# Feed-forward up projection as seven products of quadrants, with the down projection as a stage of its own

## The chip, the cores and the metric

The kernel runs on one core of a Trainium2 chip. The metric is the time of one execution on the device in microseconds (us). Three executions of the kernel before took 2954.87, 2956.52 and 2956.6 us (median 2956.52). All data are fp32. Each large matrix product is computed on TensorE from operands that are split into a high and a low part in the fp32r format: `a = ah + al`, `b = bh + bl`, and `ah*bh + ah*bl + al*bh` is summed in PSUM. One product of two tiles is therefore three matmuls.

## The reference

One layer of a transformer over 1024 tokens and 1024 channels: an input norm, a modulation, nine projections, a retention branch, a differential attention branch, their merge, and a feed-forward part. The change concerns the last part alone. Cut to that:

```python
def conv_ffn(h, w_up, conv_w, conv_b, w_down):
    u, gate = jnp.split(h @ w_up, 2, axis=-1)          # h 1024x1024, w_up 1024x5632
    u = dwconv_centred(u, conv_w, conv_b)              # 3 taps along the tokens
    return (jax.nn.gelu(u, approximate=False) * gate) @ w_down   # 2816x1024

x = layer_norm(alpha * x + g1 * y_mix, ln1_g, ln1_b)
y_ff = conv_ffn(x * (1 + sc2) + sh2, w_up, conv_w, conv_b, w_down)
x = layer_norm(alpha * x + g2 * y_ff, ln2_g, ln2_b)
```

## The kernel before

The kernel is a row of stages p0 to p6, each with pools of its own. A scheduler that works from a timeline of its own sets the order of the instructions on each engine; a semaphore wait stands wherever an instruction needs another engine's result. Engines are in order: an instruction that waits holds back what is queued behind it.

**Stage p5** (output projection, first norm). Tokens are taken in two halves `i` of 512 (four blocks of 128, `bb`) and channels in two halves `ch`. For each block, 24 matmuls `pxo` (8 channel tiles by 3) give 512 output channels. VectorE adds them to the residual (`r`, then `x0`). Once both channel halves of a block are there, `norm1` takes mean and variance on VectorE, a square root on ScalarE and a few one-column operations on VectorE; ScalarE normalises the 128x1024 block, TensorE transposes it in eight pieces (`pth`), and ScalarE copies them to `h32[i]`, the transposed input of the feed-forward part (channel tile `k` in 0 to 7, 512 tokens). When a half is complete, `hT[i][k]`, the split pair of `h32*scale + shift`, is made.

**Stage p6** (feed-forward). The 2816 inner channels are 22 tiles `f` of 128.

- `up(c0)` loads a 1024x128 block of `w_up` (`load_split`: a DMA into `wraw`, a ScalarE cast to `wh`, a VectorE subtraction to `wl`) and multiplies it with both token halves: 8 tiles by 3 by 2 halves = 48 matmuls of 512 columns into a PSUM tile of 1024 columns. `ff_tile(f)` calls it for the `u` block and for the gate block (96 matmuls), convolves and applies Gelu (two passes on ScalarE, two on VectorE, which read PSUM), multiplies with the gate, and splits the result into `fh`, `fl`.
- `down(fs)` loads the rows of `w_down` for two tiles (GpSimd multiplies them by the gate `g2`, the row `mrow`), and for eight token blocks and two column halves sums 12 matmuls `pyd` in one of two PSUM banks ("small"); VectorE adds the bank to the accumulator `acc[b]`, kept in SBUF. The last `down` takes four tiles at once, and `finish(b)` does the second norm and the store after each block.
- `down` of a pair of tiles runs between the `ff_tile` calls of the next pair, so the two projections are interleaved on TensorE.
- `init_acc` loads the normed input from DRAM (`d_x1`) into `acc` and has GpSimd multiply by `alpha*ln1_g` and add `ln1_b`: 16 operations of 128x1024. It is issued after the first `ff_tile`, and the up projection of the first tiles runs meanwhile.
- For the first two tiles `up` is called with `apart`: the first token half's matmuls stand ahead of the second half's, so that they can run before the second half is normed.

The weights go through a ring of 3 `wraw` and 4 pairs `wh`, `wl`. On the profile's page L256 is the matmul of `mm3`, L1230 that of `up` with `apart` off, L71 every `tensor_tensor`, L85 every cast, L81 every activation, L77 every `scalar_tensor_tensor`.

Of the kernel before, what the change touches and what calls it, by code (L numbers as in the profile page):

```python
# [8 lines left out]
F32 = mybir.dt.float32  # L9
# [55 lines left out]
def build(nc, tc, A, out, upto=99, dbg=None):  # L65
    top = ExitStack()
    V, S, G, PE, SP = nc.vector, nc.scalar, nc.gpsimd, nc.tensor, nc.sync
# [39 lines left out]
    d_oT = dram("d_oT", [HD, P, T])  # L107
    d_x1 = dram("d_x1", [T, D])
    d_tab = dram("d_tab", [HR, P, 896])

# [136 lines left out]

    def mm3(ps, lhs, rhs, n, start, stop, step=512):

        (wh, wl), (mh, ml) = lhs, rhs  # L250
        cuts = list(range(0, n, step))
        seq = [(wh, mh), (wh, ml), (wl, mh)]
        for i, (w, m) in enumerate(seq):
            for c in cuts:
                e = min(c + step, n)
                PE.matmul(ps[:, c:e], w, m[:, c:e], start=start and i == 0, stop=stop and i == 2)  # L256

# [560 lines left out]
    with ExitStack() as ph:  # L818
# [145 lines left out]
        for h in range(HR):  # L964
            nxt = prepare(h + 1) if h + 1 < HR else iter(())
            for c in range(NC):
# [14 lines left out]
                if h == HR - 1 and c == 2:  # L981
                    early.close()
                    open_ring("wring2", 3, 4, top, "right")
                    ws0 = w_cols(A["w_diff_out"][0], 0, 256)
# [5 lines left out]

    halves = top.enter_context(tc.tile_pool(name="halves", bufs=1))
    mrow = halves.tile([P, 2 * D], F32, name="mrow")
# [4 lines left out]
    ops = top.enter_context(tc.tile_pool(name="ops", bufs=1))  # L999
    open_big(top)  # L1000
# [109 lines left out]
    hs = misc.tile([P, 2, KT], F32, name="hs")  # L1110
    hT = []
    with ExitStack() as ph:
# [49 lines left out]
        for i in range(2):  # L1162
            for ch in range(2):
# [30 lines left out]
    with ExitStack() as ph:  # L1194
        wp = ph.enter_context(tc.tile_pool(name="p6", bufs=1))
        acc = half_pair("acc")
        acc = [acc[b // 4].rearrange("p k t -> p (k t)")[:, (b % 4) * D:(b % 4 + 1) * D] for b in range(8)]
        w_up = A["w_up"][0].rearrange("(k p) n -> p k n", p=P)
        w_dn = A["w_down"][0]

        def rows2(names):
            r = []
            for n in names:
                r.append(misc_tile("rows", 2 + len(r)))
                SP.dma_start(out=r[-1], in_=A[n].broadcast_to([P, D]))
            return r
# [10 lines left out]

        def up(c0, apart):

            h, l = load_split(w_up[:, :, c0:c0 + P])  # L1220
            pu = big_ps("pu")
            for i in range(2) if apart else (None,):
                for k in range(KT):
                    w = h[:, k * P:(k + 1) * P], l[:, k * P:(k + 1) * P]
                    if apart:
                        mm3(pu[:, i * 512:i * 512 + 512], w, hT[i][k], 512, k == 0, k == KT - 1)
                        continue
                    for at, (a, b) in enumerate(((0, 0), (0, 1), (1, 0))):
                        for j in range(2):
                            PE.matmul(pu[:, j * 512:j * 512 + 512], w[a], hT[j][k][b],  # L1230
                                      start=k == 0 and at == 0, stop=k == KT - 1 and at == 2)
            return pu

        def ff_tile(f):
            pu = up(f * P, f < 2)
            pg = up(FF + f * P, f < 2)
            cw = [pcol2[:, j * NF + f:j * NF + f + 1] for j in range(3)]
            u = misc_tile("u", f % 2)
            act(u, pu, AF.Identity, bias=pcol[:, V_CB + f:V_CB + f + 1], scale=cw[1])
            stt(u[:, 1:], pu[:, :T - 1], cw[0], u[:, 1:], ALU.mult, ALU.add)  # L1240
            stt(u[:, :T - 1], pu[:, 1:], cw[2], u[:, :T - 1], ALU.mult, ALU.add)
            act(u, u, AF.Gelu)
            tt(u, u, pg, ALU.mult)
            ah = wp.tile([P, T], F32R, name="fh", tag="fh", bufs=4)
            al = wp.tile([P, T], F32R, name="fl", tag="fl", bufs=4)
            split(ah, al, u)
            return ah, al

        def down(fs, acts, last):
            ws = [load_split(w_dn[f * P:(f + 1) * P, :], mul=mrow[:, D:]) for f in fs]  # L1250
            for b in range(8):
                cut = slice(b * P, b * P + P)
                for hf in range(2):
                    py = small_ps("pyd")
                    c = slice(hf * 512, hf * 512 + 512)
                    for i, (w, a) in enumerate(zip(ws, acts)):
                        mm3(py, (a[0][:, cut], a[1][:, cut]), (w[0][:, c], w[1][:, c]), 512, i == 0, i == len(fs) - 1)
                    tt(acc[b][:, c], py, acc[b][:, c], ALU.add)
                if last:
                    finish(b)  # L1260

        def finish(b):

            halves_of = [(slice(c, c + 512), acc[b][:, c:c + 512]) for c in (0, 512)]
            mv = wp.tile([P, 2], F32, name="mv2", tag="mv2", bufs=3)
            ln_mean_var(wp, [x for _, x in halves_of], mv, "ln2")
            if b < 7:
                rstd_shift(wp, mv[:, 0:1], mv[:, 1:2], 1, "ln2", 3)
            else:
                for c, x in halves_of:  # L1270
                    stt(x, x, mv[:, 0:1], l2[0][:, c], ALU.subtract, ALU.mult)
                rs = ln_rstd_root(wp, mv[:, 1:2], 1, "ln2s")
            for c, x in halves_of:
                if b < 7:
# [6 lines left out]

        pend = None
        for g in range(0, NF - 4, 2):
            a0 = ff_tile(g)
            if pend:
                down(*pend, False)
            else:
                with tc.issue_after(last):
                    init_acc()
            a1 = ff_tile(g + 1)  # L1290
            pend = ([g, g + 1], [a0, a1])
        g = NF - 4
        acts = [ff_tile(g)]
        down(*pend, False)
        l2 = rows2(("ln2_g", "ln2_b"))
        acts += [ff_tile(g + i) for i in range(1, 4)]
        down([g + i for i in range(4)], acts, True)
    return top

# [24 lines left out]
```

## Time and profile before

| | |
|---|---|
| median of three runs | 2956.52 us |
| the profiled execution's own time | 2954.79 us |
| its span, first to last instruction | 2953.0 us |
| TensorE busy | 2848.6 us, 96% of the span |
| VectorE, ScalarE, GpSimd busy | 1651.5, 968.3, 582.6 us |
| mean granted TensorE clock | 0.989 of full speed |
| first matmul of the up projection | 2194.16 us into the span |
| last matmul of the kernel | 2939.82 us |

The page counts a matmul from its issue to its end; matmuls are pipelined, so the distance between two starts is what one costs in a row. An idle time is put down to what ended it. "Chain" is the sequence of work that ended last, followed back from the end.

### The profile page before, as it was taken

To read this page: it belongs to the slowest core of one execution; us is meant where nothing else is said; L and a number is where in the kernel's file an instruction comes from. 1 tells how busy PE (TensorE), PEld (TensorE's weight loads), DVE (VectorE), ACT (ScalarE), POOL (GpSimd) and SP (SyncE) were. 2 spreads that over 40 slices of the span, in tenths; PEclk is the share of its full clock that TensorE was granted. 3 is DMA by queue.
4 is the path that set the end of the run, shared out by engine and by line. 5 is a ranking of instruction groups with operands and counts; after the bars stand their busy time and mean duration, and the time that the engine had idled before them with its cause. 6 is when DMAs were issued, how large, how long until landed. Compare 5 with 4: busy or idle time off the path is not lost.

```text
span 2953.0 us, 34822 instructions
## 1 busy us (share of the span) xinstructions
PE 2848.6 (96%) x13874; PEld 2378.6 (81%) x13874; DVE 1651.5 (56%) x2441; ACT 968.3 (33%) x1314; POOL 582.6 (20%) x407
## 2 busy tenths in 40 slices
PE   7999999999999999999988998999799999999998
PEld 5788888888888888888866777887677888888886
DVE  4853133200367767666689996476865444444446
ACT  4321100111354455544455544322344121112112
POOL 3321022100000000000055543233607000000014
PEclk9999999999999999999999999999999999999999
DMA  8554322422233323322143426657344111111111
GB/s 245 170 155 136 107 86 94 149 79 71 84 93 106 107 84 109 99 94 90 50 137 125 134 75 201 226 186 239 104 142 127 52 44 50 43 50 51 57 43 57
DMA packets 259170, 321.29 MB, mean 109 GB/s; under 512 B 14983, under 2 KB 192576, under 8 KB 259008
## 3 DMA queue, kind: packets, MB, share of 16 engines
q1 hardware_dynamic: 220704, 239.62, 26.3%
q10 hardware_dynamic: 38304, 79.45, 7.6%
q8 instruction: 109, 1.79, 0.3%
q14 instruction: 53, 0.43, 0.1%
HBM read 235.38 MB, written 83.62 MB: 108 GB/s over the span
## 4 chain that ended last, share of the span: by engine, by line
PE 83%; DVE 8%; DMA 4%; issue 2%; POOL 2%; ACT 1%; SPq 0%; DVEq 0%; POOLq 0%; ACTq 0%
PE pu L1230 15%; PE pg L256 12%; PE px L256 11%; PE pxn L256 11%; PE py L256 8%; PE pyd L256 7%; PE sp L706 5%; PE po L256 4%; PE pxo L256 3%; PE tp L730 2%; PE pcx L256 2%; PE pu L256 1%; DVE md L77 1%; DMA mr<-in_w_mod 1%; DVE ql L71 1%
## 5 line engine op out<-in xcount | busy, mean ns | idle before, releaser
L71 DVE TENSOR_TENSOR wl<-wraw,wh 128x1024 fp32r<-128x1024 f32 (+1 forms) x206 | 287.2, 1406 | 408.9 <-ACT wh L85 406.5
L85 ACT CAST wh<-wraw 128x1024 fp32r<-128x1024 f32 (+1 forms) x206 | 199.5, 982 | 735.8 <-PE pu L1230 337.6
L71 DVE TENSOR_TENSOR acc<-pyd,acc 128x512 f32<-128x512 f32 x160 | 110.0, 688 | 251.2 <-PE pyd L256 251.2
L709 DVE TENSOR_SCALAR_CACHE_REDUCE e<-sp 128x1280 f32<-128x1280 f32 x128 | 190.6, 1489 | 106.6 <-PE sp L706 105.9
L82 ACT ACTIVATE e<-e,m 128x1280 f32<-128x1280 f32 x128 | 175.0, 1367 | 186.1 <-DVE e L709 186.1
L1230 PE MATMUL pu<-oph,wh 128*128 128x512 f32 x640 | 201.5, 389 | 0.0
L1230 PE MATMUL pu<-opl,wh 128*128 128x512 f32 x640 | 201.5, 389 | 0.0
L1230 PE MATMUL pu<-oph,wl 128*128 128x512 f32 x640 | 200.0, 389 | 0.0
L256 PE MATMUL pg<-xH,wl 128*128 128x512 f32 x496 | 194.8, 393 | 0.0
L256 PE MATMUL pg<-xH,wh 128*128 128x512 f32 x496 | 194.8, 393 | 0.0
L256 PE MATMUL pg<-xL,wh 128*128 128x512 f32 x496 | 194.5, 392 | 0.0
L71 POOL TENSOR_TENSOR rd<-ident,wh 128x512 fp32r<-128x512 f32 x16 | 17.7, 1107 | 852.2 <-ACT wh L85 817.3
L706 PE MATMUL sp<-ks,qd 128*128 128x512 f32 (+1 forms) x768 | 174.1, 362 | 1.2 <-DVE e L709 1.2
L256 PE MATMUL py<-oph,wh 128*128 128x512 f32 x384 | 152.1, 402 | 16.0 <-DVE ga L71 11.1
L71 POOL TENSOR_TENSOR wraw<-wraw,mrow 128x1024 f32<-128x1024 f32 x22 | 53.0, 2410 | 565.6 <-DMA wraw<-in_w_down 459.8
L71 POOL TENSOR_TENSOR rp<-rp,rp 128x1024 f32<-128x1024 f32 x32 | 88.7, 2796 | 375.5 <-DVE rp L71 375.5
L256 PE MATMUL px<-xH,wh 128*128 128x512 f32 x512 | 158.7, 394 | 0.5 <-ACT xH L85 0.5
L256 PE MATMUL px<-xL,wh 128*128 128x512 f32 x512 | 159.0, 392 | 0.0
L256 PE MATMUL px<-xH,wl 128*128 128x512 f32 x512 | 158.1, 390 | 0.0
L256 PE MATMUL py<-opl,wh 128*128 128x512 f32 x384 | 152.7, 398 | 1.6 <-DVE opl L71 1.4
L256 PE MATMUL py<-oph,wl 128*128 128x512 f32 x384 | 151.6, 397 | 0.0
L256 PE MATMUL pxn<-wh,xH 128*128 128x512 f32 x384 | 149.5, 389 | 0.0
(320 smaller groups left out, 6821.6 us busy)
## 6 DMA issues: line engine op xcount, KB each, us to landing
wraw<-in_w_in SPq DMA_DIRECT2D x88, 512.0 KB, 4.0
wraw<-in_w_up SPq DMA_DIRECT2D x44, 512.0 KB, 4.1
qd<-d_qd SPq DMA_DIRECT2D x128, 128.0 KB, 3.0
mr<-in_w_mod SPq DMA_DIRECT2D x32, 512.0 KB, 4.9
ga<-d_ga SPq DMA_DIRECT2D x24, 512.0 KB, 5.5
wraw<-in_w_down SPq DMA_DIRECT2D x22, 512.0 KB, 3.6
ks<-d_kd SPq DMA_DIRECT2D x16, 640.0 KB, 6.5
d_vr<-st ACTq DMA_DIRECT2D x20, 512.0 KB, 2.7
```

The costliest lines, as they stand in the source:

```text
L71: eng.tensor_tensor(out=o, in0=a, in1=b, op=op)
L77: V.scalar_tensor_tensor(out=o, in0=a, scalar=s, in1=b, op0=op0, op1=op1)
L82: return S.activation(out=o, in_=a, func=func, bias=bias, scale=scale, accum_out=accum)
L85: S.copy(out=h, in_=x)
L256: PE.matmul(ps[:, c:e], w, m[:, c:e], start=start and i == 0, stop=stop and i == 2)
L706: st["pe"] = PE.matmul(sp[:, a:b], w, r["k"][c][:, a:b], start=part == 0, stop=part == 1).ins
L709: V.tensor_scalar(out=e, in0=sp[:, :TK], scalar1=-0.125, scalar2=None, op0=ALU.mult, op1=ALU.min, accum_out=m)
L730: PE.transpose(tp[:, k, :], a[:, k * P:(k + 1) * P], ident)
L1230: PE.matmul(pu[:, j * 512:j * 512 + 512], w[a], hT[j][k][b], start=k == 0 and at == 0, stop=k == KT - 1 and at == 2)
```

## The change

With the input cut into four quadrants (token half by channel half) and the weights into four (channel half by `u` or gate), the up projection is a product of two 2x2 block matrices, and seven products of sums of quadrants replace the eight. What the change does:

- At the end of p5 only the first token half is split directly (the quadrants "11" and "12"). At the start of p6, for each of four channel tiles, VectorE and GpSimd form the sums `s1` to `s4` in place, and ScalarE and VectorE split five of the seven operands ("22", `s1` to `s4`).
- `up_weights(f)` loads the `u` and the gate block of a tile. GpSimd forms four sums of 128x512, and three and a half pairs of 1024 columns are split (two before).
- `ff_tile(f)` runs seven products of 12 matmuls each (84 for 96). Four of them (1, 6, 7, 4) follow each other in one small PSUM bank, which ScalarE copies out after each; the other three go to a large PSUM tile, and VectorE adds them to the copies. Convolution and Gelu then read SBUF. The result `u` is written to DRAM (`d_u`).
- After all 22 tiles the pools of the up projection are closed. A new stage, p7, loads two tiles of `d_u` and of `w_down`, calls `init_acc`, and runs `down` over groups of 2, 4, 4, 4, 4 and 4 tiles. `finish` is unchanged. `apart` and the interleaving are gone.

The diff, cut to its core:

```diff
@@ end of p5
-            hT.append([op_pair() for k in range(KT)])
             for k in range(KT):
-                x, (h, l) = h32[i][:, k, :], hT[i][k]
-                act(h, x, AF.Identity, bias=hs[:, 1, k:k + 1], scale=hs[:, 0, k:k + 1])
-                last = ts(x, x, hs[:, 0, k:k + 1], hs[:, 1, k:k + 1], ALU.mult, ALU.add, G if k % 2 else V).ins
-                tt(l, x, h.bitcast(F32), ALU.subtract)
+                x = h32[i][:, k, :]
+                if i == 0:
+                    h, l = op_pair()
+                    quad["11" if k < 4 else "12"].append((h, l))
+                    act(h, x, AF.Identity, bias=hs[:, 1, k:k + 1], scale=hs[:, 0, k:k + 1])
+                ts(x, x, hs[:, 0, k:k + 1], hs[:, 1, k:k + 1], ALU.mult, ALU.add, G if k % 2 else V)
+                if i == 0:
+                    tt(l, x, h.bitcast(F32), ALU.subtract)
@@ start of p6
+        for k in range(4):
+            a11, a12, a21, a22 = h32[0][:, k, :], h32[0][:, 4 + k, :], h32[1][:, k, :], h32[1][:, 4 + k, :]
...
+            take("22", a22, op_pair())
+            tt(a22, a21, a22, ALU.add, G if k % 2 else V)
+            take("s1", a22, op_pair())
+            tt(a21, a11, a21, ALU.subtract, G)
+            tt(a11, a22, a11, ALU.subtract)
+            take("s2", a11, sum_pair())
+            take("s3", a21, sum_pair())
+            tt(a12, a12, a11, ALU.subtract, G if k % 2 else V)
+            take("s4", a12, sum_pair())
@@ up_weights
+            b1 = pair(u)
+            tt(u[:, lo], g[:, lo], u[:, lo], ALU.subtract, G)
+            tt(g[:, lo], g[:, hi], g[:, lo], ALU.subtract, G)
+            b22 = pair(g[:, hi], 512)
+            tt(g[:, hi], g[:, hi], u[:, lo], ALU.subtract, G)
+            t32 = pair(g)
+            tt(u[:, hi], u[:, hi], g[:, hi], ALU.subtract, G)
+            t14 = pair(u)
@@ ff_tile
+            def product(ps, n, first):
+                for k in range(4):
+                    mm3(ps, w[n][k], quad[sums[n]][k], 512, first and k == 0, k == 3, more=not first)
+            product(chain, 1, True)
+            S.copy(out=raw[:, t0], in_=chain)
+            product(p2, 2, True)
+            tt(raw[:, t0], raw[:, t0], p2, ALU.add)
+            product(chain, 6, False)
+            S.copy(out=g[:, t0], in_=chain)
+            product(p5, 5, True)
+            product(chain, 7, False)
+            S.copy(out=g[:, t1], in_=chain)
+            tt(g[:, t1], g[:, t1], p5, ALU.add)
+            product(chain, 4, False)
+            S.copy(out=raw[:, t1], in_=chain)
+            product(p5, 3, False)
+            tt(g[:, t0], g[:, t0], p5, ALU.add)
...
+            SP.dma_start(out=d_u[f], in_=u)
@@ the new stage p7
+        def load_act(f):
+            raw = wp.tile([P, T], F32, name="araw", tag="araw", bufs=3)
+            SP.dma_start(out=raw, in_=d_u[f])
...
+        cuts = [0, 2, 6, 10, 14, 18, NF]
+        nxt = [load_act(f) for f in range(2)], [load_down(f) for f in range(2)]
+        init_acc()
+        for at, f0 in enumerate(cuts[:-1]):
+            acts, ws = nxt
+            if at == len(cuts) - 2:
+                l2 = rows2(("ln2_g", "ln2_b"))
             else:
-                with tc.issue_after(last):
-                    init_acc()
...
+                fs = range(cuts[at + 1], cuts[at + 2])
+                nxt = [load_act(f) for f in fs], [load_down(f) for f in fs]
+            down(ws, acts, at == len(cuts) - 2)
```

TensorE at the end of p5, before the change: `pxo` is the output projection, `pth` the transposes of a normed block, `pu` the up projection. "..." stands for 40 rows of `pu`.

```order
L256 MATMUL pxo<-wl,oph 128x512
L256 MATMUL pxo<-wh,opl 128x512
L256 MATMUL pu<-oph,wh 128x512
...
L256 MATMUL pu<-oph,wl 128x512
L1138 MATMUL pth<-ident,x_16966 128x128 x8
L256 MATMUL pu<-oph,wh 128x512
L256 MATMUL pu<-opl,wh 128x512
L256 MATMUL pu<-oph,wl 128x512
L256 MATMUL pu<-oph,wh 128x512
L256 MATMUL pu<-opl,wh 128x512
L256 MATMUL pu<-oph,wl 128x512
L1138 MATMUL pth<-ident,x_16971 128x128 x8
L1138 MATMUL pth<-ident,x_16976 128x128 x8
```

The same place with the change:

```order
L257 MATMUL pxo<-wl,oph 128x512
L257 MATMUL pxo<-wh,opl 128x512
L1143 MATMUL pth<-ident,x_16970 128x128 x8
L1143 MATMUL pth<-ident,x_16975 128x128 x8
L1143 MATMUL pth<-ident,x_16980 128x128 x8
L257 MATMUL pu<-oph,wh 128x512
L257 MATMUL pu<-opl,wh 128x512
```

The 48 up matmuls that stood between the last `pxo` and the last transposes are gone from there; the transposes now follow the output projection directly.

GpSimd from the end of p5 on, before: `h` is the modulated input, `rows` the two rows of the first norm, `acc` the accumulators, `wraw` with `mrow` the weights of the down projection.

```order
L74 TENSOR_SCALAR h_16822<-h_16822,hs 128x512 x4
L74 TENSOR_SCALAR rows<-rows 128x1024 x2
L71 TENSOR_TENSOR acc_17676<-acc_17676,rows 128x1024 x4
L71 TENSOR_TENSOR acc_17677<-acc_17677,rows 128x1024
```

GpSimd at the passage from the up to the down projection with the change (`draw` is a row block of `w_down`):

```order
L71 TENSOR_TENSOR wraw<-wraw 128x512 x80
L74 TENSOR_SCALAR rows<-rows 128x1024 x2
L71 TENSOR_TENSOR draw<-draw,mrow 128x1024 x2
L71 TENSOR_TENSOR acc<-acc,rows 128x1024 x12
L71 TENSOR_TENSOR draw<-draw,mrow 128x1024
L71 TENSOR_TENSOR acc<-acc,rows 128x1024
L71 TENSOR_TENSOR draw<-draw,mrow 128x1024 x2
L71 TENSOR_TENSOR acc<-acc,rows 128x1024 x3
L71 TENSOR_TENSOR draw<-draw,mrow 128x1024 x17
```

The 16 accumulator operations moved from the start of the up projection to behind its end, with five multiplications of weights among them.

The DMAs that SyncE issues at the same passage with the change (`d_u` is the result of the up projection in DRAM, `araw` the tile it is read into):

```order
L1293 DMA d_u<-u 128x1024
L1310 DMA rows<-in_ln_b 128x1024
L1325 DMA araw<-d_u 128x1024 x2
L221 DMA draw<-in_w_down 128x1024 x2
L1319 DMA acc<-d_x_70 128x1024 x8
```

The loads of the down projection stand behind the last write of the up projection.

## Rows read from the trace of the kernel before

**Rows 1.** The page, part 1: busy time of each engine, share, instructions

```profile
PE 2848.6 (96%) x13874; PEld 2378.6 (81%) x13874; DVE 1651.5 (56%) x2441; ACT 968.3 (33%) x1314; POOL 582.6 (20%) x407
```

**Rows 2.** The page, part 4: share of the chain by engine

```profile
PE 83%; DVE 8%; DMA 4%; issue 2%; POOL 2%; ACT 1%; SPq 0%; DVEq 0%; POOLq 0%; ACTq 0%
```

**Rows 3.** The chain in order of time: start us, us, what

```profile
2262.51 21.76 PE pu L1230 x96
```

**Rows 4.** Busy us by stretch: PE, PEld, DVE, ACT, POOL, PEclk, DMA, GB/s

```profile
2194.10:2199.70 5.60, 5.60 (x26) 4.63 (x26) 4.45 (x13) 1.10 (x2) 0.00 (x0) 1.00 0.81 236
2249.70:2262.50 12.80, 12.77 (x49) 10.43 (x50) 7.70 (x5) 4.42 (x4) 12.80 (x6) 0.87 0.28 81
2284.28:2349.56 65.28, 65.28 (x289) 54.06 (x289) 27.94 (x30) 12.66 (x13) 6.72 (x3) 1.00 0.19 57
2893.50:2940.30 46.80, 44.76 (x193) 35.45 (x191) 37.09 (x58) 14.07 (x22) 26.23 (x58) 1.00 0.15 57
```

**Rows 5.** TensorE in order of time: start us, us, what, idle before

```profile
2212.82 0.39 PE L256 MATMUL pxo<-wh,opl 128*128 128x512 f32 x1
...
2228.29 0.96 PE L256 MATMUL pu<-oph,wh 128*128 128x512 f32 x3 [1.03 <-ACT oph L81]
...
2249.73 0.47 PE L256 MATMUL pu<-oph,wh 128*128 128x512 f32 x1 [4.20 <-DVE u L77]
...
2939.82 0.39 PE L256 MATMUL pyd<-wh,fl 128*128 128x512 f32 x1
```

**Rows 6.** VectorE, ScalarE, GpSimd in order of time, end of p5

```profile
2213.25 0.69 DVE L71 TENSOR_TENSOR r<-pxo,mrow 128x512 f32<-128x512 f32 x1 [0.22 <-PE pxo L256]
...
2224.17 1.25 ACT L81 ACTIVATE x<-x,nb,ln_rs 128x1024 f32<-128x1024 f32 x1
...
2228.28 0.55 DVE L74 TENSOR_SCALAR h<-h,hs 128x512 f32<-128x512 f32 x1 [4.80 <-ACT oph L81]
...
2229.53 0.77 POOL L74 TENSOR_SCALAR h<-h,hs 128x512 f32<-128x512 f32 x1 [6.84 <-ACT oph L81]
...
2230.63 1.29 DVE L71 TENSOR_TENSOR opl<-h,oph 128x512 fp32r<-128x512 f32 x2
```

**Rows 7.** VectorE beside GpSimd; last row: `acc` operations, ns min/median/max

```profile
2241.90 3.19 DVE L71 TENSOR_TENSOR wl<-wraw,wh 128x1024 fp32r<-128x1024 f32 x1 [4.78 <-ACT wh L85]
2245.01 1.27 DVE L77 SCALAR_TENSOR_TENSOR u<-pu,pcol,u 128x1023 f32<-128x1023 f32 x1
...
L71 POOL TENSOR_TENSOR acc<-acc,rows x16: 2398/2417/3391, 2239.2 to 2283.8; 128x1024 f32<-128x1024 f32 x16
```

**Rows 8.** Groups from 1950 us on, shapes apart: busy us, mean ns, idle

```profile
L71 DVE TENSOR_TENSOR wl<-wraw,wh 128x1024 fp32r<-128x1024 f32 x89 | 122.1, 1381 | 64.4 <-ACT wh L85 64.0
L85 ACT CAST wh<-wraw 128x1024 fp32r<-128x1024 f32 x89 | 92.4, 1051 | 475.1 <-PE pu L1230 337.6 <-PE pyd L256 83.1 <-PE py L256 16.6
L77 DVE SCALAR_TENSOR_TENSOR u<-pu,pcol,u 128x1023 f32<-128x1023 f32 x44 | 56.2, 1277 | 0.4
L71 POOL TENSOR_TENSOR wraw<-wraw,mrow 128x1024 f32<-128x1024 f32 x22 | 53.0, 2410 | 565.6 <-DMA wraw<-in_w_down 459.8 <-DVE acc L71 96.5 <-issue 9.3
L81 ACT ACTIVATE u<-pu,pcol,pcol 128x1024 f32<-128x1024 f32 x22 | 26.4, 1201 | 0.0
L81 ACT ACTIVATE u<-u 128x1024 f32<-128x1024 f32 x22 | 23.4, 1062 | 63.2 <-DVE u L77 63.2
L71 POOL TENSOR_TENSOR acc<-acc,rows 128x512 f32<-128x512 f32 x14 | 17.7, 1286 | 6.5 <-ACT acc L81 6.5
L71 DVE TENSOR_TENSOR ga<-py,ga 128x512 f32<-128x512 f32 x25 | 17.0, 685 | 12.1 <-PE py L256 12.1
```

**Rows 9.** DMA issues over the span: KB each, median us to landing

```profile
wraw<-in_w_down SPq DMA_DIRECT2D x22, 512.0 KB, 3.6
...
d_x<-x ACTq DMA_DIRECT2D x8, 512.0 KB, 4.8
acc<-d_x SPq DMA_DIRECT2D x8, 512.0 KB, 6.5
```

More of the change, by code (lines that the diff above doesn't have):

```diff
@@ L246, in w_cols, with mm3 @@
         return res
-    def mm3(ps, lhs, rhs, n, start, stop, step=512):
+    def mm3(ps, lhs, rhs, n, start, stop, step=512, more=False):
         (wh, wl), (mh, ml) = lhs, rhs
@@ L255, in mm3 @@
                 e = min(c + step, n)
-                PE.matmul(ps[:, c:e], w, m[:, c:e], start=start and i == 0, stop=stop and i == 2)
+                PE.matmul(ps[:, c:e], w, m[:, c:e], start=start and i == 0, stop=stop and i == 2, skip_group_check=more)
     w_mod_v = A["w_mod"][0].rearrange("(p k) n -> p k n", k=KT)
@@ L1195, in build, with sum_pair, take @@
         wp = ph.enter_context(tc.tile_pool(name="p6", bufs=1))
[L1196 to L1198 removed]
+        def sum_pair():
+            return [wp.tile([P, 512], F32R, name="sm" + n, tag="sm" + n, bufs=12) for n in "hl"]
+        for n in ("22", "s1", "s2", "s3", "s4"):
+            quad[n] = []
+        for k in range(4):
+            a11, a12, a21, a22 = h32[0][:, k, :], h32[0][:, 4 + k, :], h32[1][:, k, :], h32[1][:, 4 + k, :]
+            def take(n, x, pair):
+                split(*pair, x)
+                quad[n].append(pair)
+            take("22", a22, op_pair())
[7 more added lines that the diff above has]
+            take("s4", a12, sum_pair())
@@ new lines, in build, with up_weights, pair @@
+        halvesx.close()
+        up = ph.enter_context(tc.tile_pool(name="p6u", bufs=1, side="right"))
+        w_up = A["w_up"][0].rearrange("(k p) n -> p k n", p=P)
+        def up_weights(f):
+            raw = []
+            for c0 in (f * P, FF + f * P):
+                raw.append(ring["pool"].tile([P, 1024], F32, name="wraw", tag="wraw", bufs=ring["raws"]))
+                SP.dma_start(out=raw[-1].rearrange("p (a b) -> p a b", b=P), in_=w_up[:, :, c0:c0 + P])
+            lo, hi = slice(0, 512), slice(512, 1024)
+            u, g = raw
+            def pair(x, n=1024):
+                h = ring["pool"].tile([P, 1024], F32R, name="wh", tag="wh", bufs=ring["bufs"])
+                l = ring["pool"].tile([P, 1024], F32R, name="wl", tag="wl", bufs=ring["bufs"])
+                split(h[:, :n], l[:, :n], x)
+                return h, l
+            b1 = pair(u)
[6 more added lines that the diff above has]
+            t14 = pair(u)
+            at = {1: (b1, 0), 2: (b1, 512), 6: (t32, 512), 5: (t14, 0), 7: (t32, 0), 3: (b22, 0), 4: (t14, 512)}
+            return {n: [[x[:, o + k * P:o + k * P + P] for x in pr] for k in range(4)] for n, (pr, o) in at.items()}
@@ L1199, in build @@
+        for f in range(NF):
+            ff_tile(f)
+    opsx.close()
+    ringx.close()
+    with ExitStack() as ph:
+        wp = ph.enter_context(tc.tile_pool(name="p7", bufs=1))
         w_dn = A["w_down"][0]
+        acc = [wp.tile([P, D], F32, name="acc", tag="acc", bufs=8) for b in range(8)]
         def rows2(names):
@@ L1216, in init_acc, with load_down, down @@
                 tt(acc[b], acc[b], l1[1], ALU.add, G)
[L1218 to L1246, printed above, removed]
+        def load_act(f):
+            raw = wp.tile([P, T], F32, name="araw", tag="araw", bufs=3)
+            SP.dma_start(out=raw, in_=d_u[f])
+            ah = wp.tile([P, T], F32R, name="fh", tag="fh", bufs=8)
+            al = wp.tile([P, T], F32R, name="fl", tag="fl", bufs=8)
+            split(ah, al, raw)
             return ah, al
-        def down(fs, acts, last):
-            ws = [load_split(w_dn[f * P:(f + 1) * P, :], mul=mrow[:, D:]) for f in fs]
+        def load_down(f):
+            return load_split(w_dn[f * P:(f + 1) * P, :], pool=wp, pre="d", raws=3, bufs=8, mul=mrow[:, D:])
+        def down(ws, acts, last):
+            n = len(ws)
             for b in range(8):
```

56 lines of the change are left out of this document (31 added, 25 removed).

## The prediction, made before the change was run

> **What bounds the kernel now.** I read the page's busy times first: TensorE is busy 96% of the span [rows 1], and the chain that ended last is TensorE for 83% [rows 2]. So a matmul that goes is worth its place in the row, unless TensorE then waits for something else. The chain in order of time gives the price: one tile's 96 up matmuls take 21.76 us [rows 3], 0.2267 us each; two tiles with the down projection of two others are 288 matmuls in 65.28 us, the same 0.2267, at the full clock of 2.4 GHz [rows 4]. Then I read the stage's ends, where TensorE is not full: the passage from p5 to p6, and the tail. The last `pxo` starts at 2212.82 and the third tile at 2262.51 [rows 3, 5]; between stand 168 of the first two tiles' 192 matmuls (24 had run in 5.6 us ahead of it, rows 4), worth 38.1 us of the 49.5. So 11.4 us are lost there: transposes, a wait of 4.20 us [rows 5], and a granted clock of 0.87 (partly at 1.2 GHz) behind that wait, where 48 matmuls took 12.8 us instead of 10.9 [rows 4]. From 2262.51 on 2976 matmuls remain (20 tiles of 96, 1056 of the down projection), 674.6 us at 0.2267, which would end at 2937.1; they end at 2940.0 [rows 5], and the span 13 us later. Elsewhere in the feed-forward part TensorE waits for nothing.
>
> **What goes.** Per tile 84 matmuls instead of 96, in 22 tiles 264: 264 x 0.2267 = **59.8 us**. All operations around them exist before or are off TensorE.
>
> By the Trainium skill's "TensorE: Matmul & The Clock Gate", section "Back-to-back issue gap", an isolated 512-column matmul costs N/2.4 + 2.5 ns = 216 ns, an estimate of 57 us for the 264; the trace's 227 ns decides, and the sum goes by it.
>
> **A tile of the up projection in steady state** takes TensorE 84 x 0.2267 = 19.0 us. VectorE gets three and a half splits of 1.38, two passes of 1.28, a product of about 1.2 and three additions of 0.69 from PSUM [rows 8]: 10.7 us. ScalarE gets three and a half casts of 1.05, four copies of 512 columns (0.6, estimated as half a cast and a little), 1.20 and 1.06: 8.3 us. GpSimd gets four operations of 1.29: 5.2 us. None is near 19. The ring holds one tile's weights, so the weights of tile f+1 are made while f is multiplied. The tightest path: the pair "22" can be cast only when product 7 of the last tile has ended (5.0 us into the period); cast, subtraction, GpSimd's difference, cast, subtraction: 0.6 + 0.7 + 1.3 + 1.05 + 1.4, with waits about 11 us into the period; product 6 needs it at 13.6. The wait for the copy of the small bank is filled with the next tile's products 1 and 2, as the order of the instructions has it. I cost this at nothing; if half a microsecond a tile is late, 20 tiles cost 10.
>
> **The start of the up projection.** Before, 48 up matmuls (the second tile's and the first's first halves) lie between the last `pxo` and the last transposes. Now none does, since a tile's weights fill the ring. TensorE waits through the norm of the last block: residual at 2213.25, normalised from 2224.17 on [rows 6]. Without the 1024-wide splits of a second tile between them this path is somewhat shorter than the 15 us that it takes now until the first matmul [rows 5]: I lay it out at 12. Then products 1 and 2 can run, but 5 and 6 need the sums. Their making is a string on VectorE and GpSimd: on VectorE four scalings of 0.55, 27 operations of 512 columns at 0.60 to 0.65 [rows 6], a 1024-wide split at 1.2 and two additions from PSUM, 22 us; on GpSimd four scalings of 0.77 [rows 6] and 12 operations of 1.29 [rows 8], 18.6 us. Do they lie beside each other? A 1024-wide subtraction on VectorE that met GpSimd's `acc` operations took 3.19 us; while a pass that reads PSUM took its usual 1.27, and GpSimd's operations stretched from 2.42 to 3.39, by the 1.0 that VectorE's alone takes [rows 7]. So with both inputs in SBUF they go one after the other, whole operations. Then the string is 22 + 18.6 = 40.6 less the PSUM additions and a little overlap of the scalings: **37 us** (bounds: 26 if VectorE's work and its cross-engine waits alone count, 44 if every step of some 40 also costs 0.1 of hand-over). TensorE's last matmul of product 6 stands at its end. In 12 + 37 us, and 4 more for product 7, the second tile's casts and a low clock behind the wait as in rows 4, TensorE does 60 matmuls, 13.6 us. Lost: 53 - 13.6 = 39.4, against 11.4 before: **+28.0**. The last tile has no next tile to fill the wait for product 7's copy: **+1**.
>
> The Trainium skill's "SBUF — State Buffer", section "Who interferes with whom", says that a VectorE instruction with two SBUF inputs and a GpSimd instruction that reads SBUF exclude each other for the whole instruction, and that one with at most one SBUF input doesn't. That is what rows 7 show; the case without it is priced below as a rival.
>
> **The passage to the down projection.** Before, there is none: up and down are interleaved, and GpSimd's 16 `acc` operations run under up matmuls. Now everything of p7 lies in memory that p6 held, and SyncE's loads stand behind the last write of `d_u`. Let e be the end of the last tile's product 4; product 3 keeps TensorE until e + 2.7. The last tile's tail runs in series: copy, 1.20, 1.28, the gate sum (0.69), 1.28, 1.06, 1.2: e + 8. Its write lands about 4 us later (4.8 of the same size, rows 9): e + 12. Only then are the loads issued: two tiles of `d_u`, two row blocks of `w_down`, eight of `acc`, 0.5 MB each; one alone lands in 3.6, four issued together in 6.5 [rows 9], 1.7 to 1.8 us apart. So the first row block of weights is there at e + 19.6. GpSimd multiplies it (2.41, rows 8), ScalarE casts it (1.05): the first down matmul at about e + 23.3.
>
> That isn't what ends it. Each of the first eight token blocks has 12 matmuls in the two small banks, VectorE adds the banks to `acc[b]`, and the next block's matmuls wait for the banks. `acc[b]` is ready when GpSimd has multiplied and added it, and GpSimd works through 2 weights, 12 `acc` operations, 1, 1, 2 and 3 in that order: 21 x 2.41 = 50.6 us from e + 19.6. Into this string VectorE puts 11 or 12 splits of 1024 columns, each of which holds GpSimd up by 1.0 [rows 7]: e + 81. The third weight pair behind it (2.4, cast, subtraction) and VectorE's split backlog in the next group's first blocks cost 3 + 4: full speed begins at about e + 88, counted as if its matmuls started there, that is 85 us after product 3. In these stand 96 matmuls, 21.8 us. Lost: **+63.4** (bounds: e + 71 without any of VectorE's operations in the string, so +46; e + 98 if the `acc` operations run at 2.83, the mean of a string of them with splits between, and the first load lands 2 us later, +73).
>
> From there 960 matmuls, 217.6 us at 0.2267, and the tail as before: the 3 us of waits (192 matmuls, worth 43.5, stand in the last 46.8 us, rows 4) and 13 behind the last matmul. VectorE's additions get fewer (96 for 160) but are hidden anyway.
>
> **The sum.** -59.8 + 28.0 + 1 + 63.4 = +32.6 on the profiled execution's own 2954.79 us: 2987.4. The median of the three runs lies 1.7 above that execution. I predict **2988 us**, slower by about 1.1%.
>
> **Rivals.** (a) *GpSimd and VectorE do run beside each other.* Then the sums take 28 and GpSimd's string ends at e + 71: 2988 - 9 - 13 = 2966, still slower. For: GpSimd's median in rows 7 is undisturbed, 2.42. Against: the 3.19 and 3.39 in the same rows. (b) *The accumulators don't hold TensorE* (the other side): the passage costs only its serial chain, e + 23 and some 3.5 for the second weight pair, 24 lost in place of 63.4, and the kernel ends at 2949, faster. It decides if the first eight blocks need less than about 27 us for their 96 matmuls, which takes `acc` operations that are ready when the banks are. For: before the change these operations cost nothing. Against: that was under some 60 us of up matmuls; here 50 us of GpSimd stand against 22 of TensorE. (c) *The ring is too tight*: the pair "22", held until the last product of the tile before, delays the casts behind it in ScalarE's order, 2.5 us a tile over 20 tiles: 3038. For: before the change casts wait for TensorE in most cases (338 of 475 us of their idle time, rows 8). Against: the 2 us of slack laid out above. (d) *Fewer matmuls, but dearer ones*: products that alternate between banks at 0.24 us a matmul instead of 0.2267, 1848 of them: +25, 3013. For: nothing in the trace; the small banks of the down projection run at the same 0.2267 as the large tiles.
>
> **Chances and range.** The forecast 62%, (a) 14%, (b) 9%, (c) 9%, (d) 6%. What a measurement can tell from no change is 0.2%, 6 us. Faster by more: (b), 9%. Within: what lies between (a) and (b), 6%. Slower: 85%. The range is the forecast's own: low end 2988 with 11 less for the sums and 17 less for the passage, 2960; high end with 7, 10 and 10 for a late tile more, 3015. It takes in (a) and (d) and leaves out (b) and (c), 18%.
>
> **What would show it.** In the changed profile: 84 matmuls in 19.0 us in the middle of the up projection, else (c) or (d); a gap of some 12 us without `pu` behind the last `pxo`, and some 37 us with 60 matmuls, TensorE released by splits of the sums; a stretch of about 85 us between the last `pg` and the second group of `pyd` with `acc` on GpSimd and VectorE's `acc` additions as what ended the waits; a GpSimd string longer than 51 us by VectorE's splits. The prediction is wrong if that stretch is under 50 us, or if a tile takes more than 20.

## The result, and the profile after

The changed kernel takes 3001.75 us (median of 4 runs, 3000.07 to 3002.88) where the kernel before takes 2956.53: ratio 1.0154, 95% interval 1.0136 to 1.0171. Slower, as predicted; 2988 was 14 us too low, inside the range. The profiled execution takes 3001.59 us, its span is 2999.8. Here and in the experiments three executions that lie far above all others of their kernel are left out: 3559.89 us of the kernel before, 5692.55 in e4 and 4699.86 in e6.

The page, busy times and chain, to be read beside [rows 1, 2]:

```profile
PE 2823.7 (94%) x13610; PEld 2346.9 (78%) x13610; DVE 1740.5 (58%) x2507; ACT 1057.7 (35%) x1458; POOL 759.9 (25%) x503
...
PE 76%; DVE 12%; DMA 4%; POOL 3%; issue 3%; ACT 2%; SPq 0%; DVEq 0%; POOLq 0%; ACTq 0%
```

TensorE has exactly 264 matmuls fewer, and its share of the chain fell from 83% to 76%: time went into waits. Nineteen tiles in the middle of the up projection, busy by engine as in [rows 4]:

```profile
2296.50:2658.00 361.50, 361.50 (x1596) 299.33 (x1595) 186.70 (x190) 153.31 (x189) 133.37 (x75) 1.00 0.25 80
```

84 matmuls take 361.50 / 19 = 19.03 us, no wait, full clock: a tile costs what was predicted. GpSimd's four operations take 133.37 / 19 = 7.0 us a tile where the working put 5.2, without a cost here. The start, TensorE, then the chain's DMAs and GpSimd pieces at the passage, to be read beside [rows 5, 6]:

```profile
2210.77 0.39 PE L257 MATMUL pxo<-wh,opl 128*128 128x512 f32 x1
...
2217.79 1.97 PE L1143 MATMUL pth<-ident,x 128*128 128x128 f32 x8 [3.89 <-ACT x L81]
...
2230.44 0.50 PE L257 MATMUL pu<-oph,wh 128*128 128x512 f32 x1 [3.00 <-ACT wh L85]
...
2247.99 0.79 PE L257 MATMUL pg<-opl,wh 128*128 128x512 f32 x1 [3.61 <-DVE opl L71]
...
2257.94 0.80 PE L257 MATMUL pu<-sml,wh 128*128 128x512 f32 x1 [0.46 <-DVE sml L71]
...
2666.07 0.39 PE L257 MATMUL pg<-smh,wl 128*128 128x512 f32 x1
...
2685.61 1.22 PE L257 MATMUL pyd<-dh,fh 128*128 128x512 f32 x2 [19.16 <-ACT dh L85]
...
2698.78 0.79 PE L257 MATMUL pyd<-dh,fh 128*128 128x512 f32 x1 [5.47 <-DVE acc L71]
...
2755.94 0.80 PE L257 MATMUL pyd<-dh,fh 128*128 128x512 f32 x1 [4.74 <-DVE acc L71]
```

```profile
2671.18 3.56 DMA d_u<-u
...
2675.78 5.41 DMA draw<-in_w_down
...
2681.43 2.35 POOL draw L71
...
2684.44 2.35 POOL draw L71
2686.79 16.90 POOL acc L71 x7
...
2706.88 15.59 POOL acc L71 x5
```

The last wait for a sum in the first tile ends at 2257.94. Behind the last `pg` stand 19.16 us of serial chain, then waits for VectorE's `acc` additions, themselves held by GpSimd's `acc` operations, until 2755.94.

What was not predicted comes later. Between groups of four tiles VectorE stands like this, and TensorE (windows with columns as in [rows 4]) like that:

```profile
2800.94 0.68 DVE L71 TENSOR_TENSOR acc<-pyd,acc 128x512 f32<-128x512 f32 x1
2801.54 1.21 DVE L71 TENSOR_TENSOR fl<-araw,fh 128x1024 fp32r<-128x1024 f32 x1
2802.67 1.22 DVE L71 TENSOR_TENSOR dl<-draw,dh 128x1024 fp32r<-128x1024 f32 x1
2803.81 3.39 DVE L71 TENSOR_TENSOR fl<-araw,fh 128x1024 fp32r<-128x1024 f32 x1
2807.12 1.27 DVE L71 TENSOR_TENSOR acc<-pyd,acc 128x512 f32<-128x512 f32 x2
```

```profile
2807.86 0.50 PE L257 MATMUL pyd<-dh,fh 128*128 128x512 f32 x1 [2.76 <-DVE acc L71]
```

```profile
2795.00:2807.80 12.80, 10.09 (x45) 8.03 (x43) 12.01 (x11) 7.60 (x8) 4.97 (x2) 1.00 0.68 243
2807.80:2843.00 35.20, 35.14 (x148) 28.94 (x149) 10.90 (x15) 0.11 (x1) 7.35 (x3) 0.95 0.11 32
```

Three splits, one of 3.39 us, stand ahead of an addition that is due; TensorE waits 2.76 us, and the granted clock of the 35 us behind the wait is 0.95 (its first 6 us in part at the lower level, 1.2 GHz, the rest at full clock) where it was 1.00 ahead of it. That happens three times, 48.2 us apart.

**The account.** Take three marks of TensorE: A, the start of the last `pxo`; B, of the last up matmul; C, of the last down matmul. Between marks, what is over the count of matmuls at 0.2267 is lost. Executions differ in A by up to 9 us (2204.5 to 2213.1) through stages that the change doesn't touch, and the account leaves that scatter out; but it is one execution of each kernel, and the ratios depart from it by 2 to 4 us, mostly to the lower side. The ratios compare each kernel with executions of the kernel before that were made along with it (medians 2956.53, 2953.50 and 2954.52 us), so ratios are to be compared and not times.

| kernel | A to B, us | lost | B to C, us | lost | ratio to before, 95% interval |
|---|---|---|---|---|---|
| before (A to C) | 727.00 | 14.3 in all | | | 1 |
| changed | 455.30 | 39.1 | 320.83 | 81.4 | 1.0154 (1.0136 to 1.0171) |
| e1_no_init | 455.96 | 39.8 | 289.69 | 50.3 | 1.0052 (1.0039 to 1.0066) |
| e2_early_init | 469.48 | 53.3 | 299.12 | 59.7 | 1.0150 (1.0136 to 1.0165) |
| e3_sums_dve | 450.05 | 33.9 | 324.31 | 84.9 | 1.0149 (1.0136 to 1.0163) |
| e4_spread | 456.02 | 39.8 | 297.04 | 57.6 | 1.0078 (1.0066 to 1.0091) |
| e5_old_up | 479.9 | 6.6 | 319.8 | 80.4 | 1.0240 (1.0226 to 1.0253) |
| e6_late_init | 455.98 | 39.8 | 275.23 | 35.8 | 1.0001 (0.9992 to 1.0010) |
| e7_no_gate | 455.22 | 39.0 | 302.13 | 62.7 | 1.0091 (1.0078 to 1.0104) |
| e8_all | 450.05 | 33.9 | 275.34 | 35.9 | 0.9981 (0.9972 to 0.9989) |

Lost is, in the quadrant form, A to B less 1836 matmuls (12 of the 1848 run ahead of A), in e5 less 2088; B to C less 1056. Of the changed kernel's 81.4, 62.4 lie ahead of 2755.94 (120 matmuls are done by then; a token block takes 12 for a pair of tiles, six in each bank, and 24 for a group of four) and 19.0 behind it: 2.8 at a low clock right behind the passage (the first 39 us below), 14.0 at the borders (4.7 each: 2.76 of wait, the rest in the matmuls right behind it), 2.3 in the tail (2.9 before).

```profile
2755.94:2795.00 39.06, 39.06 (x161) 32.10 (x162) 14.62 (x17) 1.35 (x2) 9.49 (x4) 0.93 0.17 54
```

### The profile page after: what moved, and what is told of

Same layout as the page of the kernel before. It is cut to its first block, busy times and chain, and to the rows that moved or that the text cites. A ratio compares the mean times of both kernels' runs of the same rounds, so it can differ in the third digit from the quotient of the medians.

```text
span 2999.8 us, 34926 instructions
## 1 busy us (share of the span) xinstructions
PE 2823.7 (94%) x13610; PEld 2346.9 (78%) x13610; DVE 1740.5 (58%) x2507; ACT 1057.7 (35%) x1458; POOL 759.9 (25%) x503
## 3 DMA queue, kind: packets, MB, share of 16 engines
q8 instruction: 107, 1.75, 0.2%
## 4 chain that ended last, share of the span: by engine, by line
PE 76%; DVE 12%; DMA 4%; POOL 3%; issue 3%; ACT 2%; SPq 0%; DVEq 0%; POOLq 0%; ACTq 0%
PE pg L257 17%; PE pxn L257 11%; PE px L257 11%; PE pu L257 8%; PE py L257 6%; PE pyd L257 5%; PE sp L707 5%; PE po L257 4%; PE pxo L257 3%; PE tp L731 2%; POOL acc L71 2%; PE pcx L257 2%; DVE md L77 1%; DMA mr<-in_w_mod 1%; PE pS L257 1%
## 5 line engine op out<-in xcount | busy, mean ns | idle before, releaser
L71 DVE TENSOR_TENSOR wl<-wraw,wh 128x1024 fp32r<-128x1024 f32 (+1 forms) x228 | 296.2, 1306 | 482.5 <-ACT wh L85 475.0
L85 ACT CAST wh<-wraw 128x1024 fp32r<-128x1024 f32 (+1 forms) x228 | 214.0, 946 | 464.1 <-PE pu L257 134.1
L71 POOL TENSOR_TENSOR wraw<-wraw 128x512 f32<-128x512 f32 x88 | 154.9, 1761 | 262.5 <-DVE wl L71 249.1
L257 PE MATMUL pyd<-dh,fh 128*128 128x512 f32 x352 | 146.1, 416 | 56.5 <-DVE acc L71 37.3
L257 PE MATMUL pxn<-wl,xH 128*128 128x512 f32 x384 | 149.4, 389 | 0.0
L257 PE MATMUL pxn<-wh,xL 128*128 128x512 f32 x384 | 149.4, 389 | 0.0
L707 PEld LDWEIGHTS sp<-ks,qd 128*128 128x128 f32 x768 | 129.6, 188 | 23.9 <-DVE e L710 3.3
```

The lines of the kernel that those rows point to most:

```text
L71: eng.tensor_tensor(out=o, in0=a, in1=b, op=op)
L85: S.copy(out=h, in_=x)
L707: st["pe"] = PE.matmul(sp[:, a:b], w, r["k"][c][:, a:b], start=part == 0, stop=part == 1).ins
```

## The experiments

**The accumulators' start left out** (e1_no_init). In `init_acc`:

```
-                tt(acc[b], acc[b], l1[0], ALU.mult, G)
-                tt(acc[b], acc[b], l1[1], ALU.add, G)
```

> Changed kernel without the 16 GpSimd operations that scale and shift the accumulators at the start of the down projection; they start from the normed rows as loaded, so this part of the computation is left out. My theory: the passage from the last product of the up projection to the full speed of the down projection (89 us in the changed kernel) is held by GpSimd's string of 21 operations, 16 of which go. What remains is the serial chain (tail, write, load, 2.35 us multiplication, cast: first down matmul 19 us after the last product) and about 30 us for the first group's 96 matmuls and the second group's loads. Full speed some 40 us earlier: 2960 us. Rival: the passage is the round trip through DRAM and VectorE's splits and additions, GpSimd only shares their time: under 15 us gained, 2987 or more.

Measured: 31.1 us less between B and C; the ratio falls by 0.0102, 30 us. Of these, 29 are in the passage (up to the 192nd down matmul 36.2 us are lost in place of 65.2): of the 46 us behind the serial chain of 19, the accumulators' operations held 29, and not 40. Behind them stood the loads, now on the chain:

```profile
2687.97 10.18 DMA araw<-d_u
...
2714.19 4.34 DMA araw<-d_u
...
2729.94 36.12 PE pyd L257 x158
```

The rival is out (it allowed 15). The theory's size was 9 too large. Two loads of the second group's input are on the chain: one, issued behind the eight `acc` loads, lands after 10.18 us, the other is issued only at 2714.19. What each of them costs is not shown.

**The accumulators' start under the up projection** (e2_early_init). In the program, behind the tiles 4 to 11 (counted from 0):

```
+            x = up.tile([P, D], F32, name="xa", tag="xa", bufs=2)
+            SP.dma_start(out=x, in_=d_x1[b * P:(b + 1) * P, :])
+            tt(x, x, l1[0], ALU.mult, G)
+            tt(x, x, l1[1], ALU.add, G)
+            SP.dma_start(out=d_x1[b * P:(b + 1) * P, :], in_=x)
```

> Changed kernel with the accumulators' scaling and shifting done earlier: during eight tiles of the up projection GpSimd makes each block through two extra buffers and writes it back to DRAM; at the passage the accumulators are only loaded. The whole computation is there. My theory: GpSimd is idle for most of the up projection (5 us of work in a 19 us tile), so this costs nothing there and gains what leaving the work out gains: about 40 us, 2960 us, within 5 us of that run. Rival: GpSimd's 16 operations of 2.4 us exclude VectorE's splits, which delay the weights of a tile, and 8 MB more pass through the queues: TensorE waits in eight tiles, 10 to 20 us of the gain are lost, 2970 to 2980 us.

Measured: 21.7 us gained between B and C, 14.2 lost between A and B. But the operations didn't run where the program has them. GpSimd made all 16 in one stretch of 69 us, while TensorE was at the second, third and fourth tile (shortest, median and longest in ns, then first and last start in us):

```profile
L71 POOL TENSOR_TENSOR xa<-xa,l1g x8: 2383/2867/3368, 2262.4 to 2321.9; 128x1024 f32<-128x1024 f32 x8
L71 POOL TENSOR_TENSOR xa<-xa,l1b x8: 2356/2884/3387, 2267.7 to 2328.6; 128x1024 f32<-128x1024 f32 x8
```

The scheduler sets the order, and these operations need nothing that the tiles compute. So two operations a tile, which the theory priced, were not tried; whether they would be free is not shown. What was tried is a row of GpSimd that is nearly full for three tiles, and for it the rival's mechanism holds, in three tiles and not in eight: both engines stretch there, and TensorE waits for the weights. VectorE, GpSimd and TensorE in order of time:

```profile
2317.35 2.30 DVE L77 SCALAR_TENSOR_TENSOR u<-ur,pcol,u 128x1023 f32<-128x1023 f32 x1
2319.69 3.31 DVE L71 TENSOR_TENSOR wl<-wraw,wh 128x1024 fp32r<-128x1024 f32 x1
```

```profile
2316.31 2.27 POOL L71 TENSOR_TENSOR wraw<-wraw 128x512 f32<-128x512 f32 x1
2318.54 3.39 POOL L71 TENSOR_TENSOR xa<-xa,l1b 128x1024 f32<-128x1024 f32 x1
```

```profile
2317.49 0.50 PE L257 MATMUL pu<-smh,wl 128*128 128x512 f32 x1 [2.57 <-DVE wl L71]
```

A split of 1.2 us takes 3.31, a GpSimd operation of 2.41 takes 3.39, and the weights come late. By the account 7.5 us should remain; the interval shows no gain, so the total meets neither the theory's 2960 nor the rival's 2970 to 2980. The profiled execution is the shortest of the four (2989.99, the others 2995.89 to 2998.83); where those lose it is not shown, nor why the passage loses 43.8 here and 36.2 in e1.

**The sums on VectorE alone** (e3_sums_dve).

```
-            tt(a22, a21, a22, ALU.add, G if k % 2 else V)
+            tt(a22, a21, a22, ALU.add)
-            tt(a21, a11, a21, ALU.subtract, G)
+            tt(a21, a11, a21, ALU.subtract)
-            tt(a12, a12, a11, ALU.subtract, G if k % 2 else V)
+            tt(a12, a12, a11, ALU.subtract)
```

> Changed kernel with the eight additions of the input's sums that GpSimd makes put on VectorE. My theory: GpSimd's 1.29 us additions and VectorE's subtractions go one after the other, so the string of 35 us loses 8 x (1.29 - 0.62) = 5.4 us and some hand-overs: 4 to 7 us faster, 2995 to 2998 us. Rival: the two engines do run beside each other and VectorE is the longer one, so 8 x 0.62 = 5 us come on top: 3007 us.

Measured: A to B is 5.25 us shorter, as the theory has it: work that moved to the longer engine made the string shorter. The total hides it (the ratio is 0.0005 lower; that the time falls into the forecast's 2995 to 2998 is luck, as the kernel before ran 3 us faster along with it). B to C is 3.5 longer: the first two borders lose 3.2 more, the first by a wait of 4.94 us for 2.76, the second by a lower clock behind the same wait.

A shorter string would also come of fewer hand-overs between the engines. The changed kernel's trace settles that: from 2226.4 to 2259.2 VectorE is idle for 1.4 us in all, but 13 of its 32 operations there are stretched beside GpSimd, by 11.1 us together (in e3 three, by 2.2). Two of them, 0.68 us alone, and GpSimd's row beside them:

```profile
2246.20 1.74 DVE L71 TENSOR_TENSOR opl<-h,oph 128x512 fp32r<-128x512 f32 x1
2247.86 1.75 DVE L71 TENSOR_TENSOR h<-h,h 128x512 f32<-128x512 f32 x1
```

```profile
2245.82 3.25 POOL L71 TENSOR_TENSOR wraw<-wraw 128x512 f32<-128x512 f32 x2 [1.29 <-DVE wl L71]
```

The same two GpSimd operations in e3:

```profile
2244.02 14.37 POOL L71 TENSOR_TENSOR wraw<-wraw 128x512 f32<-128x512 f32 x2 [6.11 <-DVE wl L71]
```

**The splits of the following group spread** (e4_spread). From the second group on, in `down`:

```
+                    add = V.tensor_tensor(out=acc[b][:, c], in0=py, in1=acc[b][:, c], op=ALU.add).ins
+                    f, to, load = next(more, (0, [], None))
+                    if load:
+                        with tc.issue_after(add):
+                            to.append(load(f))
```

> Changed kernel in which VectorE's splits for the following group of the down projection are queued one behind each addition into an accumulator, from the second group on, instead of in a burst at the group's start. My theory: at the three borders between groups of four tiles the burst (eight splits of 1.22 us, one stretched to 3.39 beside GpSimd's multiplication) delays the additions, TensorE waits 2.76 us for a bank and then runs below full clock for some 35 us, 4.7 us a border: 14 us faster, 2988 us. Rival: the border's wait is the end of the group itself (buffers and loads that come free only then), whatever VectorE's order: no change. A second one: the lower clock behind the wait comes anyway and only the 2.76 us go: 8 us faster, 2994 us.

Measured: 23.8 us less between B and C; the ratio falls by 0.0076, 22 us. Both rivals are out. The chain's last piece, and VectorE at a border:

```profile
2730.22 192.91 PE pyd L257 x840
```

```profile
2792.60 0.69 DVE L1343 TENSOR_TENSOR acc<-pyd,acc 128x512 f32<-128x512 f32 x1 [0.90 <-PE pyd L257]
2793.21 2.85 DVE L71 TENSOR_TENSOR dl<-draw,dh 128x1024 fp32r<-128x1024 f32 x1
2795.98 0.68 DVE L1343 TENSOR_TENSOR acc<-pyd,acc 128x512 f32<-128x512 f32 x1
```

840 matmuls without a wait; the three borders lose nothing, 14.0 us less. A split still meets GpSimd (2.85), but one between two additions fits. Nearly 10 us more came in the passage (55.5 lost by the 192nd down matmul for 65.2), which I had not expected: the third group's first splits no longer stand in GpSimd's string and ahead of the second group's first additions, and the wait of 4.74 us at 2755.94 is gone.

**The separation alone** (e5_old_up). The old up projection (`up`, 96 matmuls a tile) in front of the new stage p7.

> The separation alone: the up projection of the kernel before (eight products, both halves of the input, its start with the first two tiles in halves), but with the down projection apart behind it and its input through DRAM, as in the changed kernel. My theory: the quadrants save 59.8 us and cost some 27 at the start; the passage (61 us lost) and the three group borders (17 us, of which the spread splits gave back nearly all) belong to the separation and come here too. 2956 + 61 + 17 = 3034 us, 3028 to 3040; in the trace 96 up matmuls in 21.8 us a tile, 11 us lost at the start. Rival: part of the passage or of the borders comes from the quadrant form (its ring of weights, its sums left in memory): under 3020 us.

```profile
2253.17 435.21 PE pu L1220 x1920
```

Measured: 96 matmuls take 435.21 / 20 = 21.76 us, and B to C loses 80.4, in the changed kernel 81.4 (the passage 3.9 less, the borders 2.9 more), so passage and borders belong to the separation, and the rival falls. The time is 7 below my figure (2956.5 x 1.0240 = 3027.5) because the old start loses 6.6 us here and not 11.4: without GpSimd's `acc` operations under it, the split that took 3.19 [rows 7] takes 1.22, and the wait of 4.20 [rows 5] is 1.25. From A to C the separation costs 799.7 - 727.0 = 72.7 us, and the quadrants give back 799.7 - 776.1 = 23.5 (71 and 25 by the ratios).

**The gate left out of the weights** (e7_no_gate).

```
-            return load_split(w_dn[f * P:(f + 1) * P, :], pool=wp, pre="d", raws=3, bufs=8, mul=mrow[:, D:])
+            return load_split(w_dn[f * P:(f + 1) * P, :], pool=wp, pre="d", raws=3, bufs=8)
```

> The changed kernel without GpSimd's multiplication of the down projection's weights by the gate (22 operations of 2.4 us; this part of the computation is left out). My theory: at each of the three group borders it is the split that meets this multiplication (3.3 to 3.4 us in place of 1.22) that lets the additions come late, the burst alone would just do: the waits of 2.76 us go or fall under 1 us, 12 to 17 us; and the passage loses 5 of the 21 operations of GpSimd's string, 12 to 15 us. Together 2972 to 2978 us. Rival: the burst of eight splits is what comes ahead of the additions: the border waits stay over 2 us and the time is 2986 to 2990 us.

VectorE and TensorE at the first border:

```profile
2789.01 1.22 DVE L71 TENSOR_TENSOR dl<-draw,dh 128x1024 fp32r<-128x1024 f32 x1
2790.14 1.22 DVE L71 TENSOR_TENSOR fl<-araw,fh 128x1024 fp32r<-128x1024 f32 x1
2791.28 0.68 DVE L71 TENSOR_TENSOR acc<-pyd,acc 128x512 f32<-128x512 f32 x1
```

```profile
2792.01 0.50 PE L257 MATMUL pyd<-dh,fh 128*128 128x512 f32 x1 [0.58 <-DVE acc L71]
```

Measured: the same burst, but no split over 1.22 at the borders, and the three waits are 0.58 and 0.59 us; the borders lose 2.7 us in place of 14.0. So it takes both, the burst (e4) and the meeting with GpSimd (e7). In the passage 7 us went where I expected 12 to 15, 3.9 of them in the serial chain, which has a multiplication less. What holds the rest is not the five operations: seven of VectorE's splits stand ahead of an addition, six of them stretched to 3.4 us by turns with GpSimd's `acc` operations, and the wait for that addition lasts 18.45 us. Two rows of these splits, and TensorE:

```profile
2695.85 3.40 DVE L71 TENSOR_TENSOR dl<-draw,dh 128x1024 fp32r<-128x1024 f32 x1
...
2709.04 6.65 DVE L71 TENSOR_TENSOR fl<-araw,fh 128x1024 fp32r<-128x1024 f32 x2
```

```profile
2716.34 0.80 PE L257 MATMUL pyd<-dh,fh 128*128 128x512 f32 x1 [18.45 <-DVE acc L71]
```

The total (ratio lower by 0.0063, 19 us) stays short of the forecast by that.

**The accumulators started late** (e6_late_init; e8_all has the sums of e3 too). With the spread splits; in the program in the first group, and behind each block of the third:

```
+                    if at == 0:
+                        S.copy(out=acc[b][:, c], in_=py)
+                        continue
...
+            tt(x, x, l1[0], ALU.mult, G)
+            tt(x, x, l1[1], ALU.add, G)
+            tt(acc[b], acc[b], x, ALU.add, G)
```

> The changed kernel with the spread splits, and with the accumulators' start moved: the first group's sums are copied from the banks by ScalarE, and the scaled and shifted normed rows are made and added by GpSimd during the third group, in the steady state of the down projection. The whole computation is there. My theory: GpSimd's 16 operations held the passage; taken out of it, and not put into the up projection, where they delayed the weights of eight tiles, they are free. Lost in the passage 27 us (19 of serial chain, the rest the loads of the second group) in place of 61, and 17 us less at the borders: 2950 us. Rival: the 24 operations of GpSimd in the third group hold VectorE's splits and additions up as in the up projection, TensorE waits there: 2960 to 2970 us. A second one: the passage is held by loads and casts and gains under 15 us: 2965 to 2970 us.

> The last kernel but one (spread splits, accumulators started late) with the sums' additions on VectorE as well. My theory: the terms add up, as each stands at another place of TensorE's row: 5 us below that kernel, 2945 us, which is under the 2956 us of the kernel before. Rival: they don't add up; what is gained at the start or in the passage is lost again at the next wait (a tile's weights, the second group's loads): 2955 us or more, no better than before.

Measured: 35.8 us lost between B and C in place of 81.4, and with the sums on VectorE A to B is again 5.9 shorter. Here the terms add up: e8 is 0.0020 below e6, 6 us, at 0.9981 (0.9972 to 0.9989) of the kernel before. That is some 5 us, where I expected 11, and at the edge of the 0.2% that the prediction says a measurement can tell: from A to C the profiled executions differ by 1.6 us alone (725.4 for 727.0), though the ratios lie below the account for most of the other kernels too. What TensorE still waits for between B and C in the last kernel (total us, times, longest):

```profile
PE pyd L257 <- ACT dh L85: 19.1, 1, 19.1
PE pyd L257 <- DVE acc L1345: 2.9, 7, 1.0
PE pyd L257 <- DVE dl L71: 2.6, 2, 1.5
PE pyd L257 <- ACT acc L1343: 2.5, 3, 1.0
```

The serial chain through DRAM, 19.1, is most of what is left. The second rival of e6 is out, the first shows in small. Of the missing 5 us, 3 are a passage of 30 us for the 27 assumed, and 3.7 are lost in the third and fourth group (five waits of 0.3 and slower matmuls), which lose nothing in e4. GpSimd's 24 late operations lie beside the splits there; they ran from within the second group to the end of the fourth. The eight additions among them, in e8:

```profile
L71 POOL TENSOR_TENSOR acc<-acc,xa x8: 2394/3337/3373, 2763.4 to 2839.9; 128x1024 f32<-128x1024 f32 x8
```

## Why the prediction was right, and where not

*What goes*: 264 matmuls at 0.2267, a tile in 19.03 us. Right; rivals (c) and (d) fall by that.

*The start*, +28.0, and +1 for the last tile: measured 39.1 - 11.4 = 27.7 for both, of which 1.0 is the last tile's. Right in size and in its parts: the first product begins 12.6 us behind the last `pxo` (12), and product 6's last matmul starts at 2258.54, where 2210.77 + 12 + 37 = 2259.8 comes out of the working. Twelve up matmuls run ahead of A, which the working had not. Rival (a) is refuted by e3 and by the stretched operations shown there: with two inputs in SBUF the engines don't run beside each other. The working took VectorE's four scalings at 0.55, though; they have one input in SBUF, and three of them took 0.93 to 1.00 us beside GpSimd's scalings.

*The passage*, +63.4: measured 62.4, and 2.8 of low clock behind it, 65.2. The last product 4 ends at e = 2663.6 (one product of 2.72 ahead of B's end); first row block at e + 17.6 (19.6 predicted, with 1.7 to 1.8 us between two loads, which no row of the kernel before shows), first down matmul at e + 22.0 (23.3), GpSimd's 21 operations from 2681.43 to 2741.70, 60.3 us (61.6), twelve of them stretched, by 11.1 us together (11 or 12 by 1.0 each), full speed at e + 92.4 with 120 matmuls done (88 with 96). The mechanism is the predicted one, and its terms hold to 2 us each; that the size agrees to 1 us is luck, as their misses cancel: GpSimd's string begins 1.8 earlier and is 1.3 shorter, and what follows it costs 8.9 and not 3 + 4. The cause is shown by e1 and e6; rival (b) needed accumulators that don't hold TensorE, and where they don't, in e6, the passage loses 30 us and not the 24 of (b). So a bound that I had not priced lay right behind: e1 gives back 29 us in the passage, not 40, and then meets the loads.

*What failed* is "From there 960 matmuls, 217.6 us at 0.2267, and the tail as before". I counted VectorE's split backlog once, in the passage, and took the steady state behind it for free because VectorE's share is small. But there are buffers for two groups, and those of the group that ends come free all at once, so the splits come in a burst at each border, one of them beside GpSimd's multiplication. Three borders of 4.7 us, 14.0 together, are nearly all of the 14.2 us that the sum was short on the span (32.6 against 46.8); the smaller misses (-1.3 at the start, -1.0 and +2.8 at the passage, -0.6 in the tail) cancel. e4 and e7 show both halves of that cause.

The sum as measured, on the span: -59.8 + 27.7 + 65.2 + 14.0 - 0.6 = 46.5; the spans differ by 46.8.

Two slips of the working change no conclusion: 2987.4 and 1.7 make 2989, not 2988; and the same e + 71 is worth 17 us in the passage's bound and 13 in rival (a).

## What to carry to other kernels

Saved matmuls are worth their full price only where TensorE has no wait; two stages that were interleaved have to be priced with everything that ran under them, here 72.7 us against 23.5. A steady state with a small busy share still stalls when its buffers come free in groups: read the order on the helping engine at each border, and put its bulk work between the operations that others wait for. Work of GpSimd was free in this kernel only where VectorE's operations with both inputs in SBUF had slack. And work that is moved has to be looked up in the trace: in e2 it ran three tiles long at the start and not where the program has it.

## What the runs showed of the hardware that was not expected

In e3 the first of two GpSimd additions of 512 columns took 13.02 us, 2244.02 to 2257.04, beside a row of 20 VectorE operations of 0.68 us without a gap that ends at 2255.92; the second, behind it, took 1.28. GpSimd did not get a share there, it waited for the end of the row. In the changed kernel the same two took 3.25 us, in a row of VectorE that has no gap either: there two of VectorE's operations gave way (1.74 and 1.75). What decides which of the two happens is not shown.

And the same wait of TensorE, 2.76 us, did not always cost the same. At the first border of the changed kernel 148 matmuls behind it took 35.20 us at a granted clock of 0.95, 1.6 more than at 0.2267; at the second border of e3 141 took 35.00 at 0.91, 3.0 more; at the first border of e1 the clock stayed at 1.00:

```profile
2779.23:2814.40 35.17, 35.17 (x155) 29.13 (x156) 11.62 (x15) 1.74 (x2) 7.33 (x3) 1.00 0.11 32
```

Behind e7's wait of 0.58 us it stayed at 1.00 too.
